# Pair sums of weight tiles made when both raw tiles are rounded, raw tiles rounded seven steps behind their loads, one addition two steps later

## The chip, the cores and the metric

The kernel runs on one core of one Trainium2 chip. A core has five engines that run at once, each with an in-order queue of its own: TensorE (PE, the matmuls), VectorE (DVE), ScalarE (ACT), GpSimd (POOL) and SyncE (SP, which here issues the DMAs). An instruction that waits for another engine or for a DMA holds up all that stands behind it in its queue. The metric is the device time of the program in microseconds.

## The reference

One inference step of one decoder layer: 1024 prompt tokens and 32 sampled tokens, model width 1024, float32. The input projection `p = rmsnorm(x) @ w_in + b_in` feeds two mixers of four heads each (an mLSTM and an HGRN2), an output projection follows, then a gated feed-forward. Cut to what matters here, the HGRN2 half:

```python
fr = f_raw
f = lb + (1.0 - lb) * sigmoid(fr)            # forget gate
kk = (1.0 - lb) * sigmoid(-fr)               # key
q, v = heads(silu(q_raw)), heads(i_raw)
# by chunks of 64 tokens: o = q*exp(b) @ S + (masked, decayed q k^T) @ v;  S carried on
out = headnorm(o) * silu(g_raw)
```

`f_raw`, `q_raw`, `i_raw`, `g_raw` are columns of `p`: for each head h, four weight tiles of 128 columns (f, q, v, g), 1024 rows each.

## The kernel before, in words

**Products.** A float32 product is made of three matmuls of rounded operands: every operand X is kept as `hi` (X rounded to fp32r, which ACT makes) and `lo` (X - hi, the "rest", made by POOL for weight tiles and by DVE for the others), and PE adds hi*hi + hi*lo + lo*hi (lines 179 to 181). A weight tile is 128 x 1024: two halves of 512 columns, each with four k-steps of 128.

**Blocks of tokens.** The tokens lie in three blocks, 0 (288 columns), 1 and 2 (384 each). For heads 0 to 2 of the HGRN2 half, the weights of two tiles (a pair: f and q, or v and g) on blocks 1 and 2 form a 2 x 2 by 2 x 2 block product, which is done with seven products P1 to P7 of four k-steps (twelve matmuls) in place of eight (`strassen_units`). The order on PE is P1, P2, P5, P6, P3, P7, then a plain unit of block 0 with the next pair's first tile (24 matmuls of 288 columns), then P4, then a plain unit with the next pair's second tile. There are six pairs, (h, 0) and (h, 1) for h = 0, 1, 2. P1, P2 and P4 read the rounded raw tiles. P5, P6, P3 and P7 read four sums of raw halves, S1, S2, S4 and S3, each rounded and split like a tile.

**Banks.** The seven products use three PSUM banks: P1 in 0, P2 in 1, P5 in 2, P6 onto bank 0, P3 onto bank 2, P7 and P4 onto bank 0. So P6 must come after the addition that reads P1 (`add`, L1156 from `p2`), P3 after the evacuation of P5 (`p5`, ACT L1152), P7 after that of P6.

**The weights' way.** `load` issues a DMA of a raw tile (512 KB, L105, into one of two buffers "raw"). `split` rounds it on ACT (L96) and has POOL make the rest (L97), half by half. `pairs_split` makes the sums in place in the two raw tiles on DVE (L139, L142, L147, L153), rounds them on ACT (L134), makes their rests on DVE (L137), and loads the next pair's raw tiles into the two buffers as soon as each is free. Rounded tiles and rests have five buffers each (`NW`); a pair takes four, two raw tiles and two tiles of sums.

**The order of the work** is that in which the program is written out. PE's matmuls are emitted unit by unit; after every second k-step and after every unit `hook()` runs one step of each active helper (a Python generator): `split`, `pairs_split`, and `mix_b`, the HGRN2 mixer of a head and a block. A helper's `yield n` puts off its next piece by n steps. So a step is some six matmuls, and a helper's instructions stand in each engine's queue where the step falls. `next_splits(ui)` starts the split of a tile, or `pairs_split`, at the unit that `t_split` gives. In code, `virt` holds the two tiles of sums of a pair with its two raw tiles; `first` and `last_u` are the first and last unit that reads a tile.

`mix_b` builds a chunk's decayed products by doubling levels: DVE multiplies q and k by decays (L865, L867: `qB`, `kB`, `qw`, `ck`) and the decays with each other (L873), DVE puts a level's product into place (L853, L882), PE makes small matmuls (L846, L924, L929), ACT copies (L870, L871, L915). Then PE transposes v and k (L945, L948), ACT and DVE copy them (L954, L955), PE makes the state's update (L964), DVE adds it to the state C (L972, L974), PE makes the output (L984, L986, the latter with C), ACT squares it (L992), and the norm goes on (L551, L556, L997, L1002). A mixer of one block runs while the units of another are multiplied.

Of the kernel before, what the change touches and what calls it, by code (L numbers as in the profile page):

```python
# [13 lines left out]
OP = mybir.AluOpType  # L14
# [26 lines left out]
def hybrid_step(ctx: ExitStack, tc: tile.TileContext, i, o):  # L41
# [18 lines left out]
    def start(gen, key, wait=1):  # L60
        active.append([gen, key, wait])

    def hook():
        for e in list(active):
            e[2] -= 1
            if e[2] > 0:
                continue
            try:
                e[2] = next(e[0]) or 1
            except StopIteration:  # L70
                active.remove(e)
                done.add(e[1])
# [13 lines left out]
    def split(t, pool):  # L86
        while t not in raws or (t and t - 1 not in his):
            yield 1
        hi = his[t] = wp.tile([128, 1024], F32R, tag="whi", name="whi", bufs=NW)
        lo = los[t] = wp.tile([128, 1024], F32R, tag="wlo", name="wlo", bufs=NW)  # L90
        n, raw = tile_n[t], raws[t]
        for c in range(0, n, 512):
            if c:
                yield 2
            s = slice(c, c + 512)
            nc.scalar.activation(hi[:, s], raw[:, s], AF.Copy)  # L96
            (nc.gpsimd if pool else nc.vector).tensor_tensor(lo[:, s], raw[:, s], hi[:, s].bitcast(F32), op=OP.subtract)  # L97
        for x in nexts.get(t, ()):
            load(x)

    tile_n = {}

    def wtile(src, n=1024):
        def f(raw):
# [18 lines left out]
    def pairs_split(tb, ta, raw_a, raw_b):  # L123

        while ("w", raw_b) not in done:
            yield 1
        ra, rb = raws[raw_a], raws[raw_b]
        a11, a12, a21, a22 = ra[:, 0:512], ra[:, 512:1024], rb[:, 0:512], rb[:, 512:1024]

        def rnd(t, s, src):  # L130
            if t not in his:
                his[t] = wp.tile([128, 1024], F32R, tag="whi", name="whi", bufs=NW)
                los[t] = wp.tile([128, 1024], F32R, tag="wlo", name="wlo", bufs=NW)
            nc.scalar.activation(his[t][:, s], src, AF.Copy)  # L134
# [4 lines left out]
        nc.vector.tensor_tensor(a22, a21, a22, op=OP.add)  # L139
# [7 lines left out]
        nc.vector.tensor_tensor(a11, a22, a11, op=OP.subtract)  # L147
# [992 lines left out]
    def swin(h, pair):  # L1140

        n0, n1 = pair
        tags = {"f": ("ngb", 2), "qb": ("cq", 2), "vb": ("v", 2), "g": ("go", 3)}
        bj = {"f": None, "qb": V_BIN + 16 + h, "vb": V_BIN + 24 + h, "g": V_BIN + 28 + h}

        def put(name, b, ps):
            t = S[name, h, b] = tl(tags[name][0], 384, tags[name][1])
            j = bj[name]
            if j is None:
                nc.scalar.activation(t, ps[:, :384], AF.Copy)  # L1150
            else:
                nc.scalar.activation(t, ps[:, :384], AF.Identity, bias=col(j))  # L1152

        def add(name, b, ps):
            t = S[name, h, b]
            nc.vector.tensor_tensor(t, t, ps[:, :384], op=OP.add)  # L1156
# [29 lines left out]
    ts_, virt = {}, {}  # L1186

    def pair_tiles(h, j):
        ta, tb = wtile(wa[17 + 4 * h + 2 * j]), wtile(wa[17 + 4 * h + 2 * j + 1])
        ts_[h, 2 * j], ts_[h, 2 * j + 1] = ta, tb  # L1190
        if h < H - 1:
            for _ in range(2):
                tiles.append(None)
            virt[tb + 1] = (tb + 1, tb + 2, ta, tb)
            virt[tb + 2] = None

    XF = {"P1": (0, 0, "B11"), "P2": (0, 512, "B21"), "P3": (3, 512, "B22"), "P4": (1, 512, "T4"), "P5": (2, 512, "T1"),
          "P6": (3, 0, "T2"), "P7": (2, 0, "T3")}
    for h in range(H):
        for j in range(2):  # L1200
            pair_tiles(h, j)
# [4 lines left out]
    def strassen_units(h, j, posts, mid, end):  # L1206
        evs = swin(h, (("f", "qb"), ("vb", "g"))[j])
        ta = ts_[h, 2 * j]
        for p, bk in (("P1", 0), ("P2", 1), ("P5", 2), ("P6", 0), ("P3", 2), ("P7", 0), ("P4", 0)):
            if p == "P4":  # L1210
                mid()
            d_, coff, b_ = XF[p]
            need = {"P5": "S1", "P6": "S2", "P3": "S4", "P7": "S3"}.get(p)
            unit(ta + d_, (Op(b_, 0), Op(b_, 1)), 4, evs[p], coff=coff, post=posts.get(p), need=need and (need, ta + 2),
                 bank=pmb(bk), acc=p in ("P6", "P3", "P7", "P4"))
        end()

# [702 lines left out]
            nexts[ta] = nexts.pop(ra) + nexts.pop(rb)  # L1920
    t_split, prev = [], 0
    for t in range(n_t1):
        e = max(prev, last_u[t + 1 - NW] + 1 if virt.get(t) else 0, first[t] - 8, last_u[t - NW] + 1 if t >= NW else 0)
        assert e <= first[t], (t, e, first[t])
        t_split.append(e)
        prev = e
# [324 lines left out]
```

## Time and profile before

| what | value |
|---|---|
| median of 3 runs | 1449.21 us (1448.50 to 1449.81) |
| the profiled execution: its time | 1452.79 us |
| the profiled execution: span in the trace | 1451.0 us |
| mean granted PE clock in it | 0.965 |
| PE busy | 1347.2 us, 93% of the span |
| DVE, ACT, POOL busy | 940.0, 584.9, 600.8 us (65%, 40%, 41%) |
| the stage of the six pairs | first sum starts at 294.7 us, last rest of a sum at 517.8 us |
| time on the chain that ended last | PE 69%, DVE 15%, ACT 5%, DMA 5% |

PE is busy nearly all the time over the whole kernel; in the stage of the six pairs it is not, and the shares of the whole span say nothing of that. In the views, a row of waits gives who waited, for whom, us in total, how often and the longest; a row of a timeline gives start, us, engine, line, operation and, in brackets, the idle time before it and what ended it; a row of a tile gives ns at least, in the median and at most.

### The profile page before, as it was taken

The numbers are of one execution on the slowest core, as the hardware profiler recorded it, in microseconds if no ns is written. First come the engines' busy times: TensorE is split into PE (matmuls) and PEld (weight loads), VectorE is DVE, ScalarE is ACT, GpSimd is POOL, SyncE is SP. The second block draws the span as 40 slices with busy tenths as digits, with TensorE's granted clock in tenths as the row PEclk, the third lists the DMA queues.
The fourth block names the chain that finished last, engine by engine and source line by source line (L and its number), as shares of the span: only waits on it lengthen the run. The fifth ranks groups of instructions, "written<-read, shape, count | busy, mean of one in ns | idle before, by whom it ended". The sixth has DMA issues, their size and how long they took to land.

```text
span 1451.0 us, 29523 instructions
## 1 busy us (share of the span) xinstructions
PE 1347.2 (93%) x11528; PEld 1308.4 (90%) x11528; DVE 940.0 (65%) x2158; ACT 584.9 (40%) x1367; POOL 600.8 (41%) x566
## 2 busy tenths in 40 slices
PE   6989999988788879989998999999999999999996
PEld 6878999877788768889998999999999999999995
DVE  6877777665666646664548567756666236777775
ACT  5655444233434334432344444544554341222232
POOL 5323213221211213312345665666566574444434
PEclk9989999999898989999999999999999999999998
DMA  6224323231010133444354666666765258888843
GB/s 217 87 67 152 102 82 93 88 110 39 20 43 20 43 118 139 137 140 147 119 196 125 220 223 236 239 207 218 248 237 191 75 183 330 288 290 282 292 168 120
DMA packets 118724, 229.71 MB, mean 158 GB/s; under 512 B 11680, under 2 KB 72120, under 8 KB 118072
## 3 DMA queue, kind: packets, MB, share of 16 engines
q1 hardware_dynamic: 118152, 227.55, 46.0%
q8 instruction: 91, 1.49, 0.5%
q14 instruction: 49, 0.40, 0.1%
q10 hardware_dynamic: 432, 0.27, 0.1%
HBM read 153.33 MB, written 74.45 MB: 157 GB/s over the span
## 4 chain that ended last, share of the span: by engine, by line
PE 69%; DVE 15%; ACT 5%; DMA 5%; issue 4%; POOL 2%; SPq 0%; POOLq 0%; DVEq 0%; ACTq 0%
PE mx L1524 15%; PE mm L1524 9%; PE mm L179 8%; PE mm L181 8%; PE mm L180 8%; PE mx L1747 7%; PE mm L1747 4%; PE so L1524 3%; DMA raw<-in_wA 2%; DMA rg<-d_ff 2%; PE mx L701 1%; PE mx L846 1%; PE so L1747 1%; ACT whi L96 1%; DVE wlo L137 1%
## 5 line engine op out<-in xcount | busy, mean ns | idle before, releaser
L179 PE MATMUL mm<-HI,whi 128*128 128x384 f32 (+2 forms) x1064 | 348.8, 328 | 17.3 <-ACT go L1152 9.2
L181 PE MATMUL mm<-HI,wlo 128*128 128x384 f32 (+2 forms) x1064 | 334.3, 314 | 1.3 <-POOL wlo L97 1.3
L180 PE MATMUL mm<-LO,whi 128*128 128x384 f32 (+2 forms) x1064 | 334.5, 314 | 0.8 <-DVE LO L1257 0.4
L97 POOL TENSOR_TENSOR wlo<-raw,whi 128x512 fp32r<-128x512 f32 x90 | 120.2, 1344 | 259.7 <-ACT whi L96 215.4
L179 PEld LDWEIGHTS mm<-HI,whi 128*128 128x128 f32 x1064 | 205.7, 193 | 23.9 <-ACT go L1152 10.3
L180 PEld LDWEIGHTS mm<-LO,whi 128*128 128x128 f32 x1064 | 206.1, 194 | 1.9 <-POOL LO L279 0.7
L181 PEld LDWEIGHTS mm<-HI,wlo 128*128 128x128 f32 x1064 | 205.8, 193 | 1.8 <-POOL wlo L97 1.8
L1453 POOL TENSOR_TENSOR wlo<-S,whi 128x512 fp32r<-128x512 f32 x78 | 110.4, 1421 | 89.4 <-ACT whi L1452 84.9
L1524 PE MATMUL mx<-T,whi 128*128 128x264 f32 x640 | 118.2, 284 | 0.0
L1524 PEld LDWEIGHTS mx<-T,whi 128*128 128x128 f32 x640 | 99.0, 188 | 0.0
L1577 POOL TENSOR_TENSOR LO<-rg,HI 128x528 fp32r<-128x528 f32 x52 | 70.6, 1367 | 66.3 <-ACT HI L1576 66.2
L1524 PE MATMUL mx<-HI,whi 128*128 128x264 f32 x320 | 91.1, 285 | 0.2 <-ACT u L1532 0.2
L1524 PE MATMUL mx<-HI,wlo 128*128 128x264 f32 x320 | 90.9, 284 | 0.0
L1524 PE MATMUL mx<-T,wlo 128*128 128x264 f32 x320 | 90.9, 284 | 0.0
L1524 PE MATMUL mx<-LO,whi 128*128 128x264 f32 x320 | 90.7, 283 | 0.0
L1665 DVE TENSOR_TENSOR fh<-fr,fh 128x512 fp32r<-128x512 f32 x80 | 68.0, 850 | 34.0 <-ACT fh L1660 33.7
L1751 DVE TENSOR_TENSOR X<-X,mx 128x264 f32<-128x264 f32 x160 | 65.5, 425 | 26.9 <-PE mx L1747 26.3
L1452 ACT ACTIVATE whi<-S 128x512 fp32r<-128x512 f32 x80 | 50.3, 630 | 71.0 <-DVE S L1441 67.2
L1576 ACT ACTIVATE HI<-rg 128x528 fp32r<-128x528 f32 x52 | 32.3, 641 | 105.1 <-PE mx L1747 31.7
L96 ACT ACTIVATE whi<-raw 128x512 fp32r<-128x512 f32 x90 | 54.2, 622 | 50.1 <-DMA raw<-in_wA 50.1
L1524 PE MATMUL mm<-HI,wlo 128*128 128x264 f32 x240 | 68.2, 284 | 0.0
L1524 PE MATMUL mm<-HI,whi 128*128 128x264 f32 x240 | 68.2, 284 | 0.0
(584 smaller groups left out, 3684.7 us busy)
## 6 DMA issues: line engine op xcount, KB each, us to landing
d_wf<-fh SPq DMA_DIRECT2D x60, 512.0 KB
rg<-d_ff SPq DMA_DIRECT2D x42, 528.0 KB
raw<-in_wA SPq DMA_DIRECT2D x31, 512.0 KB
whi<-d_wf SPq DMA_DIRECT2D x29, 512.0 KB
wlo<-d_wf SPq DMA_DIRECT2D x28, 512.0 KB
raw<-in_wgu SPq DMA_DIRECT2D x24, 512.0 KB
d_ff<-sg SPq DMA_DIRECT2D x40, 264.0 KB
rg<-in_wgu SPq DMA_DIRECT2D x20, 512.0 KB
```

What stands on the lines that cost most here:

```text
L96: nc.scalar.activation(hi[:, s], raw[:, s], AF.Copy)
L97: (nc.gpsimd if pool else nc.vector).tensor_tensor(lo[:, s], raw[:, s], hi[:, s].bitcast(F32), op=OP.subtract)
L179: nc.tensor.matmul(ps[:, :n], wh, rh[:, k, :], start=(k == 0 and not u["acc"]), stop=False, skip_group_check=sk)
L180: nc.tensor.matmul(ps[:, :n], wh, rl[:, k, :], start=False, stop=False, skip_group_check=sk)
L181: nc.tensor.matmul(ps[:, :n], wl, rh[:, k, :], start=False, stop=(k == nk - 1), skip_group_check=sk)
L1452: nc.scalar.activation(hi[:, s], t, AF.Copy)
L1453: (nc.vector if dve else nc.gpsimd).tensor_tensor(lo[:, s], t, hi[:, s].bitcast(F32), op=OP.subtract)
L1524: nc.tensor.matmul(ps[:, :QN], a[:, w], b_[:, kk, c], start=new and kk == 0 and x == 0, stop=kk == 3 and x == 2, skip_group_check=True)
L1577: (nc.vector if dve else nc.gpsimd).tensor_tensor(lw, src, h.bitcast(F32), op=OP.subtract)
L1665: nc.vector.tensor_tensor(lw, src, h.bitcast(F32), op=OP.subtract)
L1747: nc.tensor.matmul(ps[:, :QN], a[:, w], b_[k][:, cs], start=new and k == 0 and x == 0, stop=k == 1 and x == 2, skip_group_check=True)
L1751: nc.vector.tensor_tensor(y, y, ps[:, :QN], op=OP.add)
```

## The change

It moves instructions; none is added or taken away, and the same values are computed.

- `pairs_split` is started by `split` of the pair's second raw tile, as soon as that is rounded, and makes all four sums then. It waits for a mark ("free", tile), which `next_splits` sets where it started `pairs_split` before, and only then rounds the sums, in the order S2, S4, S1, S3 (S1, S2, S4, S3 before). S2 and S4 lie in the first of the two tiles of sums now, S1 and S3 in the second.
- `hook` counts its calls. The two loads that `pairs_split` issues note the count plus 7 in `landed`, and `split` rounds such a tile no earlier than at that count.
- the addition that reads P1 is started two steps after P2's evacuation instead of with it.

```diff
     def hook():
+        hooks[0] += 1
...
     def split(t, pool):
         while t not in raws or (t and t - 1 not in his):
             yield 1
+        while hooks[0] < landed.get(t, 0):
+            yield 1
...
         for x in nexts.get(t, ()):
             load(x)
+        if virt.get(t + 2):
+            start(pairs_split(*virt[t + 2]), ("w", t + 2))
...
         nc.vector.tensor_tensor(a22, a21, a22, op=OP.add)
         yield 1
-        rnd(tb, right, a22)
         nc.vector.tensor_tensor(a21, a11, a21, op=OP.subtract)
         yield 1
-        rest(tb, right, a22)
-        done.add(("S1", tb))
-        yield 1
         nc.vector.tensor_tensor(a11, a22, a11, op=OP.subtract)
+        yield 1
+        nc.vector.tensor_tensor(a12, a12, a11, op=OP.subtract)
+        yield 1
+        while ("free", tb) not in done:
+            yield 1
         rnd(ta, left, a11)
         yield 1
         rest(ta, left, a11)
         done.add(("S2", tb))
-        yield 1
-        nc.vector.tensor_tensor(a12, a12, a11, op=OP.subtract)
         rnd(ta, right, a12)
         yield 1
         rest(ta, right, a12)
         done.add(("S4", tb))
         x0, x1 = nexts[ta]
         load(x0)
-        yield 1
+        landed[x0] = hooks[0] + 7
+        rnd(tb, right, a22)
+        yield 1
+        rest(tb, right, a22)
+        done.add(("S1", tb))
         rnd(tb, left, a21)
...
         load(x1)
+        landed[x1] = hooks[0] + 7
...
         def p2(ps):
             put(n0, 1, ps)
-            add(n0, 1, pm[0])
+            start(later(n0, pm[0]), ("later", n0, h), 2)
...
             if nxt in virt:
-                if virt[nxt]:
-                    start(pairs_split(*virt[nxt]), ("w", nxt))
+                done.add(("free", nxt))
```

The order on PE is the same, instruction by instruction. Three places in the other queues, first ACT in pair (0,1), from P2's evacuation on. `whi<-raw` of L134 rounds a sum, of L96 a raw tile; `v<-mm` and `go<-mm` evacuate P2, P5 and P6. Before:

```order
L96 ACTIVATE whi<-raw 128x512
L1152 ACTIVATE v<-mm,vec 128x384
L134 ACTIVATE whi<-raw 128x512
L870 ACTIVATE qw<-qB 128x24x8
L871 ACTIVATE ck<-kB 128x24x8
L96 ACTIVATE whi<-raw 128x512 x2
L1152 ACTIVATE go<-mm,vec 128x384
L992 ACTIVATE kt,sm<-mx 128x128 x2
L96 ACTIVATE whi<-raw 128x512
L1152 ACTIVATE v<-mm,vec 128x384
```

After the change, where L101 rounds a raw tile, L1163 evacuates, L881, L882 and L1003 are L870, L871 and L992 of before, L926 is L915, and L814 and L815 make the next block's key `ck` and gate `ngb`:

```order
L1163 ACTIVATE v<-mm,vec 128x384
L881 ACTIVATE qw<-qB 128x24x8
L882 ACTIVATE ck<-kB 128x24x8
L1163 ACTIVATE go<-mm,vec 128x384
L101 ACTIVATE whi<-raw 128x512
L1003 ACTIVATE kt,sm<-mx 128x128 x2
L1163 ACTIVATE v<-mm,vec 128x384
L926 ACTIVATE AT_124<-AD_126 32x3x32 x4
L101 ACTIVATE whi<-raw 128x512 x2
...
L815 ACTIVATE ngb<-ngb,vec 128x384
L101 ACTIVATE whi<-raw 128x512
```

The evacuations of P2 and P5 now stand ahead of the first rounding of a raw tile, and the last of the four roundings stands behind `ngb`.

The DVE near the end of the same pair, from the addition of P3 on (`v<-v,mm`); `go<-go,mm` adds P7, and `qB`, `kB` are the mixer's last level, which PE's L948 transposes. Before:

```order
L1156 TENSOR_TENSOR v<-v,mm 128x384
L807 TENSOR_SCALAR ngb<-ngb,omlb,lb 128x384
L808 TENSOR_SCALAR ck<-ck,omlb 128x384
L1156 TENSOR_TENSOR go<-go,mm 128x384
L865 TENSOR_TENSOR qB<-qB,wib 128x3x64
L867 TENSOR_TENSOR kB<-kB,wib 128x3x64
```

After, with L146, L148 and L150 three of the four sums of the next pair:

```order
L1167 TENSOR_TENSOR v<-v,mm 128x384
L818 TENSOR_SCALAR ngb<-ngb,omlb,lb 128x384
L819 TENSOR_SCALAR ck<-ck,omlb 128x384
L146 TENSOR_TENSOR raw<-raw 128x512
L1167 TENSOR_TENSOR go<-go,mm 128x384
L876 TENSOR_TENSOR qB<-qB,wib 128x3x64
L878 TENSOR_TENSOR kB<-kB,wib 128x3x64
L884 TENSOR_TENSOR wib<-wib 128x3
L148 TENSOR_TENSOR raw<-raw 128x512
L150 TENSOR_TENSOR raw<-raw 128x512
```

The sums have come in between the mixer's instructions of the pair before, the first of them ahead of `go`, `qB` and `kB`.

The DVE in pair (1,0), around the addition that reads P1 (`ngb<-ngb,mm`); L137 and L144 make the rest of a sum. Before, as the piece between the mixer's level ahead and the copy of `kt`:

```order
L137 TENSOR_TENSOR wlo<-raw,whi 128x512
L153 TENSOR_TENSOR raw<-raw 128x512
L137 TENSOR_TENSOR wlo<-raw,whi 128x512
L1156 TENSOR_TENSOR ngb<-ngb,mm 128x384
L865 TENSOR_TENSOR qB<-qB,wib 128x3x64
L867 TENSOR_TENSOR kB<-kB,wib 128x3x64
L873 TENSOR_TENSOR wib<-wib 128x3
L137 TENSOR_TENSOR wlo<-raw,whi 128x512
```

After:

```order
L144 TENSOR_TENSOR wlo<-raw,whi 128x512
L876 TENSOR_TENSOR qB<-qB,wib 128x3x64
L878 TENSOR_TENSOR kB<-kB,wib 128x3x64
L884 TENSOR_TENSOR wib<-wib 128x3
L1167 TENSOR_TENSOR ngb<-ngb,mm 128x384
L966 COPY kt<-mx 128x384
```

The products `qB` and `kB` no longer stand behind the addition.

More of the change, by code (lines that the diff above doesn't have):

```diff
@@ L61, in start @@
         active.append([gen, key, wait])
+    hooks, landed = [0], {}
     def hook():
+        hooks[0] += 1
         for e in list(active):
@@ L99, in split @@
             load(x)
-    tile_n = {}
+        if virt.get(t + 2):
+            start(pairs_split(*virt[t + 2]), ("w", t + 2))
+    tile_n, virt = {}, {}
     def wtile(src, n=1024):
@@ L140, in pairs_split @@
         yield 1
-        rnd(tb, right, a22)
         nc.vector.tensor_tensor(a21, a11, a21, op=OP.subtract)
         yield 1
-        rest(tb, right, a22)
-        done.add(("S1", tb))
+        nc.vector.tensor_tensor(a11, a22, a11, op=OP.subtract)
         yield 1
-        nc.vector.tensor_tensor(a11, a22, a11, op=OP.subtract)
+        nc.vector.tensor_tensor(a12, a12, a11, op=OP.subtract)
+        yield 1
+        while ("free", tb) not in done:
+            yield 1
         rnd(ta, left, a11)
@@ L1166, in p2, with later @@
             put(n0, 1, ps)
-            add(n0, 1, pm[0])
+            start(later(n0, pm[0]), ("later", n0, h), 2)
+        def later(name, ps):
+            add(name, 1, ps)
+            return
+            yield
         def p5(ps):
@@ L1184, in swin @@
         return {"P1": lambda ps: None, "P2": p2, "P5": p5, "P6": p6, "P3": p3, "P7": p7, "P4": p4}
-    ts_, virt = {}, {}
+    ts_ = {}
     def pair_tiles(h, j):
@@ L1193, in pair_tiles @@
                 tiles.append(None)
[L1194 to L1198, printed above, removed]
+            virt[tb + 1] = None
+            virt[tb + 2] = (tb + 2, tb + 1, ta, tb)
+    XF = {"P1": (0, 0, "B11"), "P2": (0, 512, "B21"), "P3": (2, 512, "B22"), "P4": (1, 512, "T4"), "P5": (3, 512, "T1"),
+          "P6": (2, 0, "T2"), "P7": (3, 0, "T3")}
     for h in range(H):
@@ L1213, in strassen_units @@
             need = {"P5": "S1", "P6": "S2", "P3": "S4", "P7": "S3"}.get(p)
-            unit(ta + d_, (Op(b_, 0), Op(b_, 1)), 4, evs[p], coff=coff, post=posts.get(p), need=need and (need, ta + 2),
+            unit(ta + d_, (Op(b_, 0), Op(b_, 1)), 4, evs[p], coff=coff, post=posts.get(p), need=need and (need, ta + 3),
                  bank=pmb(bk), acc=p in ("P6", "P3", "P7", "P4"))
@@ L1922, in hybrid_step @@
     for t in range(n_t1):
-        e = max(prev, last_u[t + 1 - NW] + 1 if virt.get(t) else 0, first[t] - 8, last_u[t - NW] + 1 if t >= NW else 0)
+        e = max(prev, last_u[t + 1 - NW] + 1 if t in virt and not virt[t] else 0, first[t] - 8, last_u[t - NW] + 1 if t >= NW else 0)
         assert e <= first[t], (t, e, first[t])
```

## The prediction

> **What bounds the kernel now.** Two views come first: how often the tensor engine (PE) is busy, and whom it waits for. The change touches only the stage in which six pairs of weight tiles are multiplied by seven products, between 295 and 531 us. The waits of PE from 309 to 531 us (waiter, releaser, us in total, times, longest):
>
> ```profile
> PE mx L948 <- DVE kB L867: 11.9, 2, 6.0
> PE mm L179 <- ACT go L1152: 9.2, 3, 4.0
> PE mx L986 <- DVE C L972: 8.6, 3, 2.9
> PE mm L179 <- DVE cq L532: 4.7, 1, 4.7
> ...
> PE mm L179 <- ACT ngb L804: 1.1, 1, 1.1
> ```
>
> The first four groups make 34.4 us, and the releasers named are evacuations and products of the mixer, not the weights. So the next question is what held ScalarE (ACT) and VectorE (DVE) up. ACT's first wait from 286 to 560 us, by length:
>
> ```profile
> ACT whi L96 <- DMA raw<-in_wA: 49.2, 11, 5.6
> ```
>
> ACT waits 11 times, 4.5 us each, for a weight tile that is still on its way (L96 rounds a raw tile). The chain of waits shows one such place, in the pair that ends at 448 us (start, us, what):
>
> ```profile
> 429.83 3.25 DMA raw<-in_wA
> ...
> 433.11 0.63 ACT whi L96
> 433.74 0.48 ACT v L1152
> 434.21 0.02 issue
> 434.24 0.55 DVE v L1156
> 434.79 0.21 DVE C L972
> ...
> 437.83 3.45 DMA raw<-in_wA
> ...
> 441.84 0.57 ACT go L1152
> 442.42 0.04 issue
> 442.46 0.69 PE mm L179
> ```
>
> The last rest (L137) of a raw tile frees its buffer, the load of the next tile goes out and takes 3.3 us (3.5 the second time), and ACT's queue already has that tile's rounding at its head. Everything behind it (v, go, then on the DVE v and C) waits with it. **The bound of this stage is a load in the middle of two in-order queues**, twice in each pair. In six windows around these places (start:end, us; busy us and instructions of PE, weight loads, DVE, ACT, POOL; granted PE clock):
>
> ```profile
> 309.70:327.00 17.30, 11.44 (x84) 10.20 (x83) 11.24 (x32) 9.50 (x25) 6.86 (x7) 0.80 0.24 79
> 352.10:368.00 15.90, 10.45 (x99) 9.21 (x99) 7.70 (x26) 8.10 (x22) 6.17 (x6) 0.79 0.17 54
> 391.50:404.30 12.80, 6.53 (x65) 5.50 (x63) 5.11 (x10) 3.96 (x10) 3.93 (x4) 0.73 0.25 82
> 431.80:448.60 16.80, 11.26 (x87) 9.84 (x87) 8.30 (x26) 8.09 (x22) 6.83 (x6) 0.70 0.14 46
> 472.30:486.10 13.80, 7.87 (x71) 7.16 (x70) 5.64 (x12) 4.74 (x11) 5.13 (x5) 0.75 0.23 76
> 511.00:530.00 19.00, 12.08 (x91) 10.95 (x91) 8.17 (x26) 8.09 (x22) 6.17 (x6) 0.75 0.33 107
> ```
>
> The windows last 95.6 us together and PE is busy in 59.6 of them: **36.0 us idle**. The clock is low too. Busy time times (1 - clock), window by window, is 2.3 + 2.2 + 1.8 + 3.4 + 2.0 + 3.0 = **14.6 us**. What the twelve loads cost is thus up to 50.6 us.
>
> **The change part by part.**
>
> *Later rounding of raw tiles.* A raw tile is now rounded at least seven steps behind its load. A step is six matmuls of a product, and six of 384 columns take 1.17 us at full clock (368.43 to 369.60):
>
> ```profile
> 368.43 0.45 PE L179 MATMUL mm<-HI,whi 128*128 128x384 f32 x1
> ...
> 369.60 0.29 PE L179 MATMUL mm<-HI,whi 128*128 128x288 f32 x1
> ```
>
> Seven steps are about 8 us against the 3.3 us of a load, so I let all eleven waits of L96 go. The order of ACT after the change bears it out: v and go, which stood behind the rounding, stand ahead of it. Gain: the 50.6 us, less what takes its place.
>
> *Pair sums early.* The same four sums, 24 roundings and 24 rests are done, with the same tiles loaded, so busy time does not change. The sums move to before the pair and overwrite the raw tile, so the first of them (L146 in the change) must wait for POOL's last rest of that tile. That is a **new wait in the middle of the DVE's queue**. Its rows:
>
> ```profile
> L97 POOL TENSOR_TENSOR wlo<-raw,whi x25: 1262/1281/1565, 287.0 to 526.2; 128x512 fp32r<-128x512 f32 x25
> ...
> L139 DVE TENSOR_TENSOR raw<-raw x6: 683/1092/1494, 294.7 to 501.0; 128x512 f32<-128x512 f32 x6
> ```
>
> In pairs (0,1) and (1,1) the sum of the next pair stands ahead of the go addition and the products qB, kB for which PE's L948 waits. I follow ACT and PE from the end of product P6 (call it 0). The rows of before for (0,1):
>
> ```profile
> 363.75 0.59 ACT L1152 ACTIVATE v<-mm,vec 128x384 f32<-128x384 f32 x1
> 364.21 1.14 ACT L915 ACTIVATE AT<-AD 32x96 f32<-32x96 f32 x4
> ...
> 366.53 0.62 ACT L804 ACTIVATE ngb<-ngb,vec 128x384 f32<-128x384 f32 x1
> ...
> 369.80 0.56 DVE L1156 TENSOR_TENSOR go<-go,mm 128x384 f32<-128x384 f32 x1 [1.70 <-PE mm L181]
> ...
> 370.54 0.35 DVE L867 TENSOR_TENSOR kB<-kB,wib 128x192 f32<-128x192 f32 x1
> ...
> 367.78 0.34 PE L924 MATMUL mx<-qw,ck 128*32 128x32 f32 x9
> ...
> 371.04 0.52 PE L948 MATMUL mx<-ident,kB 128*128 128x128 f32 x3 [0.16 <-DVE wib L873]
> ```
>
> ACT: v 0.59, AT 1.14, two roundings 1.26 (0.63 each, by L96 in the chain), two copies about 0.7, ck and ngb 1.24 (0.62 each), the last rounding 0.63: 5.6. POOL's rest 1.28: 6.9. DVE: sum 0.68, go 0.56, qB and kB 0.7 (0.35 each): 8.8. PE: 18 matmuls 3.5, then from L924 to L948 as before, 371.04 - 367.78 = 3.26 less its wait of 0.16, 3.1: 6.6, at which it wants L948. **The new wait is about 2.2 us**, and 0.4 us of it would be there without the sum (ACT's ngb is done at 4.9; its scaling on the DVE, about 0.9 as two such instructions, and go and the products follow: 7.0). Bounds: 0, if POOL is done when ACT is, and 6.1 if three queued rests of 1.28 follow each other first. What does such a wait cost in clock? The 2.85 us waits at L986 (the third row above) were followed, the first time, by these two windows:
>
> ```profile
> 355.50:358.00 2.50, 2.49 (x53) 2.06 (x56) 2.43 (x10) 1.15 (x3) 0.20 (x2) 0.71 0.03 7
> 358.00:362.50 4.50, 2.28 (x25) 1.92 (x17) 0.27 (x1) 0.77 (x2) 1.41 (x2) 0.78 0.39 117
> ```
>
> 2.49 x 0.29 + 2.28 x 0.22 = 1.2 us were lost behind 2.85 us of wait. I take 1.2 (and 0 as the other end), so 3.4 us at each of two places: **6.8 back**, between 0 and 14.6. Pair (2,1) has no sums ahead: **0.4 back**.
>
> The Trainium skill, "TensorE: Matmul & The Clock Gate", section "Why this matters for your kernels", says that only gaps of more than about 3 us bring the clock down. The row of 355.5 us speaks against it, with 0.71 granted after 2.85 us. By the rule the two places would give back 4.4 instead of 6.8 us, and the time would be 2.4 us lower than mine.
>
> In pairs (0,0), (1,0), (2,0) the sums stand between the mixer's level products, POOL's four rests run beside them, and a sum next to POOL took 1.49 us instead of 0.68 (row L139). No row shows how much of this reaches PE. I take one sum ahead of the products and one such stretch, 0.68 + 0.81 = 1.5 us per place, **4.5 back**, between 0 (PE's slack covers it) and 9 (twice that).
>
> *Rounding of sums in the order S2, S4, S1, S3.* P5 needs S1, now third. The three roundings stand back to back with inputs long ready, where before ACT and DVE passed each sum to and fro. Three roundings and three rests need some 3.9 us (0.63 and, like a sum, 0.68 each) and P5 is two products (24 matmuls, 4.7 us) away: nothing. If that cover were gone it would be one rounding and one rest, 1.3 us a pair.
>
> *One addition two steps later.* P6 accumulates onto the bank that it reads, so it must be done before P6. It has 1.17 us of P5's second half and the mixer's matmuls for its 0.55 us: nothing; uncovered, 0.55 us a pair, 3.3 in all.
>
> *Loads.* Both loads of a pair go out earlier, with the same bytes. On SP they pass one store of states in (0,0); nobody waits for it there.
>
> *What stays in pair (0,0).* P5 waited 4.7 us for cq (fourth wait above), the end of a DVE chain that starts with ACT's ngb. ACT before:
>
> ```profile
> 310.12 0.63 ACT L96 ACTIVATE whi<-raw 128x512 fp32r<-128x512 f32 x1 [4.52 <-DMA raw<-in_wA]
> ...
> 312.46 0.49 ACT L804 ACTIVATE ngb<-mm,vec 128x288 f32<-128x288 f32 x1
> ```
>
> ck and ngb read a product that lies on PE just ahead of P1. PE's wait for ngb (1.1 us, fifth row above) came after P1, whose twelve matmuls take 2.3 us, and ended with ngb at 312.95; so the product was there by 312.95 - 1.1 - 2.3 = 309.6, before the load was. Without the rounding ahead of them, ck and ngb (0.49 and as much) are done at 310.6, some 2.3 us sooner, and with a rounding of sums (0.63, behind ngb in ACT's queue) moved forward too the chain is some 2.7 sooner. PE arrives 1.1 us sooner as well, so 4.7 - 2.7 + 1.1 = 3.1 us of wait stay, and with them I leave 1.5 of that window's 2.3 us of clock: **4.6 back**, between 3 and 7.
>
> **Sum.** 50.6 - 6.8 - 0.4 - 4.5 - 4.6 = 34.3 us. The profiled execution took 1452.8 us (span 1451.0), which gives 1418.5 for one like it; it stands 3.6 us above the median of the runs, 1449.2, so the forecast is **1415 us**. With all that comes back at its least (3) the gain is 47.6, 1401.6; at its most (14.6 + 1 + 9 + 7 = 31.6) it is 19, 1430.
>
> **The rivals.**
>
> *The waits just vanish:* POOL is done in time and PE meets nothing new, 1402 us or a little less. For it: none of PE's long waits names a weight tile. Against it: ACT's queue is full from P6 to the last rounding. 0.14.
>
> *DVE behind POOL becomes the next bound:* the sum's wait is twice mine, the level products slip at every pair, and PE pays clock again. The gain falls to 10 to 25 us, 1424 to 1439. For it: the DVE is the busiest of the helpers in the six windows, 46 us against ACT's 42. 0.16.
>
> *The change doesn't do what it says:* steps are counted, not time, and a step can pass without a matmul when a wait is being filled; then the rounding still meets its load, and the time stays at 1449. Against it: PE's order is the same instruction by instruction. 0.04.
>
> *Slower:* the same wait of the DVE's sum for POOL, at the five places where sums stand, (0,0) to (2,0), costs more than it frees. It decides from 50.6 / 5 = 10.1 us a place; at 12 us (POOL held by PE's old tiles, PE by the DVE behind it) the time is 1449.2 + 9.4 = 1459. Against it: the upper bound above is 6.1. 0.04.
>
> **How the numbers follow.** My forecast (gain 25 to 44) has 0.58, the rivals 0.14, 0.16, 0.04 and 0.04, and 0.04 is left for a gain beyond 50. About 0.2% is what a measurement can tell from no change. Faster by more than that: 0.58 + 0.14 + 0.16 + 0.04 = 0.92; within 0.04; slower 0.04. The range takes the bounds of the unknown costs and reaches a little into the second rival: 1401 to 1434.
>
> **What the profile after would show.** ACT's waits for raw tiles from in_wA between 286 and 530 us: near 0 instead of 49 us. L986 waiting for C and the main matmuls for go: gone. L948 waiting for kB: about 2 us in (0,1) and (1,1), none of 6 us in (1,0) and (2,0), with the sum waiting for POOL just ahead. P5 of (0,0) still waiting some 3 us for cq. The clock in the stretches of the six windows near 0.9 or above. If ACT still waits for loads, the first step is wrong; if a wait for POOL of over 5 us stands on the DVE at each sum, the second.

## The result and the profile after

| what | before | changed |
|---|---|---|
| median (runs of one comparison) | 1448.86 us (1447.89 to 1449.81) | 1411.99 us (1411.00 to 1413.13) |
| ratio to before | | 0.9746, interval 0.9729 to 0.9763 |
| the profiled execution: its time | 1452.79 us | 1411.00 us |
| mean granted PE clock | 0.965 | 0.98 |
| PE busy | 1347.2 us (93%) | 1331.9 us (95%) |

The forecast was 1415 us, 1401 to 1434. By medians the change saves 36.9 us; the two profiled executions differ by 41.8, because that of before lies 3.9 us above its median and that of the change 1.0 below.

The first step was that no rounding of a raw tile waits for its load. The view of line L101 (L96 before) in the changed kernel, from 286 to 530 us, gives the roundings and then, under "until", what its engine sat idle for; before, it was the DMA for 49.2 us:

```profile
L101 ACT ACTIVATE whi<-raw x30: 613/622/669, 308.0 to 522.6; 128x512 fp32r<-128x512 f32 x30
its engine sat idle before it (us, times) until:
who waited for it (us, times):
```

The list under "until" is empty. PE's waits after the change, 286 to 540 us (waiter, releaser, us, times, longest; L959 is L948 of before, L940 L929, L857 L846):

```profile
PE mx L959 <- DVE wib L884: 7.5, 3, 2.9
PE mx L940 <- DVE wib L884: 3.1, 2, 1.6
PE mx L857 <- DVE wib L884: 2.9, 4, 1.0
PE mx L940 <- ACT qB L881: 2.0, 2, 1.0
PE mx L857 <- ACT sg L1172: 1.6, 3, 0.7
```

PE's waits for go and cq are gone, and C is down from 8.6 to 0.9 us. L959 still waits for kB (`wib` L884 is the small product behind it): 2.86 us in (0,1), 2.87 in (1,1), 1.80 in (2,1).

PE's order is the same in both kernels, so the start of one and the same matmul can be compared. How far the change is ahead, worked out from the two timelines of PE (starts before and after, us):

| up to | before | after | ahead by | gained or given back |
|---|---|---|---|---|
| first pair's sums | 296.86 | 295.18 | 1.7 | |
| end of window 1, (0,0) | 325.69 | 315.27 | 10.4 | +8.7 |
| start of (0,1) | 334.63 | 325.92 | 8.7 | -1.7 |
| end of window 2 | 366.81 | 348.91 | 17.9 | +9.2 |
| behind L959's wait | 374.47 | 362.01 | 12.5 | -5.4 |
| end of window 3, (1,0) | 408.05 | 387.07 | 21.0 | +8.5 |
| start of (1,1) | 417.90 | 398.73 | 19.2 | -1.8 |
| end of window 4 | 448.07 | 418.87 | 29.2 | +10.0 |
| behind L959's wait and the next pair's start | 469.61 | 444.78 | 24.8 | -4.4 |
| end of window 5, (2,0) | 482.66 | 450.01 | 32.7 | +7.8 |
| start of (2,1) | 498.53 | 466.95 | 31.6 | -1.1 |
| end of window 6 | 530.15 | 487.10 | 43.1 | +11.5 |
| behind L959's wait | 533.85 | 492.44 | 41.4 | -1.6 |

The six places of the loads give 55.7 us, and 16.0 come back between them: 39.7 in this stage. Predicted were 50.6 and 16.3. Neither sum holds what lies ahead of the first row. Up to 290 us, where nothing differs, the two executions are already 2.8 us apart; 1.1 of that are lost at 295 us, where PE's L602 waits 1.0 us for the DVE, a wait that is found neither in the kernel before nor in the one with the delay alone.

Where the most comes back, in (0,1), the timeline of the changed kernel (start, us, engine, line, operation, and in brackets the idle time before it and what ended it):

```profile
346.91 0.58 ACT L1163 ACTIVATE v<-mm,vec 128x384 f32<-128x384 f32 x1 [1.98 <-PE mm L192]
...
351.39 0.61 DVE L818 TENSOR_SCALAR ngb<-ngb,omlb,lb 128x384 f32<-128x384 f32 x1 [1.84 <-ACT ngb L815]
...
351.93 1.53 DVE L819 TENSOR_SCALAR ck<-ck,omlb 128x384 f32<-128x384 f32 x1
351.96 1.28 POOL L102 TENSOR_TENSOR wlo<-raw,whi 128x512 fp32r<-128x512 f32 x1 [0.17 <-ACT whi L101]
...
353.20 1.11 POOL L886 TENSOR_TENSOR qw<-cq,ngb 128x384 f32<-128x384 f32 x1
353.38 1.48 DVE L146 TENSOR_TENSOR raw<-raw 128x512 f32<-128x512 f32 x1
...
355.51 0.35 DVE L878 TENSOR_TENSOR kB<-kB,wib 128x192 f32<-128x192 f32 x1
...
356.00 0.87 PE L959 MATMUL mx<-ident,kB 128*128 128x128 f32 x3 [2.86 <-DVE wib L884]
```

From the end of P6 (346.9) the last rest of POOL ends at 6.3 (6.9 predicted), kB at 8.95 (8.8), and L959 wanted it at 6.2 (6.6). The time that the DVE lost is not written as a wait for POOL, though: ck's scaling takes 1.53 us where its median is 0.42, and ends 0.2 us behind POOL's rest; the sum takes 1.48 where its median is 0.69, and ends 0.55 us behind POOL's L886, as if it had begun only then. What the wait costs behind it, by the granted clock of the same kernel (start:end, us; busy of PE, weight loads, DVE, ACT, POOL; clock):

```profile
356.00:358.00 2.00, 2.00 (x53) 1.63 (x54) 1.49 (x3) 0.25 (x1) 0.00 (x0) 0.50 0.04 8
358.00:360.00 2.00, 2.00 (x10) 2.00 (x10) 1.99 (x6) 0.67 (x2) 0.00 (x0) 0.50 0.00 0
360.00:362.00 2.00, 2.00 (x10) 1.99 (x9) 0.81 (x3) 0.00 (x0) 0.00 (x0) 0.50 0.00 0
```

Six busy microseconds at a granted clock of 0.50 lose 3 us, by the same estimate that had given me 1.2.

### The profile page after: what moved, and what is told of

Same layout as the page of the kernel before. It is cut to its first block, busy times and chain, and to the rows that moved or that the text cites. A ratio compares the mean times of both kernels' runs of the same rounds, so it can differ in the third digit from the quotient of the medians.

```text
span 1409.2 us, 29523 instructions
## 1 busy us (share of the span) xinstructions
PE 1331.9 (95%) x11528; PEld 1297.2 (92%) x11528; DVE 935.5 (66%) x2158; ACT 582.7 (41%) x1367; POOL 601.6 (43%) x566
## 4 chain that ended last, share of the span: by engine, by line
PE 69%; DVE 16%; ACT 7%; issue 4%; POOL 2%; DMA 2%; POOLq 0%; ACTq 0%; DVEq 0%; SPq 0%
PE mx L1540 16%; PE mm L1540 9%; PE mx L1763 8%; PE mm L190 7%; PE mm L192 7%; PE mm L191 7%; PE mm L1763 5%; PE so L1540 3%; ACT whi L101 1%; PE so L1763 1%; PE mx L712 1%; DMA rg<-d_ff 1%; PE mx L857 1%; POOL LO L1593 1%; ACT HI L294 1%
## 5 line engine op out<-in xcount | busy, mean ns | idle before, releaser
L1469 POOL TENSOR_TENSOR wlo<-S,whi 128x512 fp32r<-128x512 f32 x78 | 109.7, 1411 | 92.3 <-ACT whi L1468 89.2
L1681 DVE TENSOR_TENSOR fh<-fr,fh 128x512 fp32r<-128x512 f32 x80 | 66.5, 832 | 34.3 <-ACT fh L1676 34.1
L567 POOL TENSOR_TENSOR sm<-sm,mhalf 128x3 f32<-128x3 f32 (+2 forms) x26 | 23.0, 883 | 106.6 <-DVE sm L562 73.6
```

Source lines behind the costliest of these rows:

```text
L1469: (nc.vector if dve else nc.gpsimd).tensor_tensor(lo[:, s], t, hi[:, s].bitcast(F32), op=OP.subtract)
L1681: nc.vector.tensor_tensor(lw, src, h.bitcast(F32), op=OP.subtract)
```

## The experiments

Medians and ratios are to the kernel before, measured on the same chip in the same comparison. The changed kernel's interval is 0.9729 to 0.9763.

**The parts alone.** First the delay without the early sums: `landed` and the wait in `split` are put into the kernel before, and nothing else.

```diff
     def hook():
+        hooks[0] += 1
...
         while t not in raws or (t and t - 1 not in his):
             yield 1
+        while hooks[0] < landed.get(t, 0):
+            yield 1
...
         load(x0)
+        landed[x0] = hooks[0] + 7
...
         load(x1)
+        landed[x1] = hooks[0] + 7
```

> The kernel before, with only the raw tiles rounded seven steps behind their loads; the sums are still made inside the pair, in the old order. Theory A (the load at the head of ACT's queue was the cost): ACT's 49 us of waits for in_wA go to near 0, the waits of PE for go (L179, 9.2 us) and C (L986, 8.6) go, and the time is 1411 to 1420. Theory B (the delay needs the early sums as well: without them the roundings of the sums, each waiting for the DVE, 25 us in all, still stand between the evacuations, and the next pair's sums now start later): the waits for in_wA go, but PE waits for rounded sums or raw tiles instead, and the time is 1425 to 1445.

Measured: 1407.26 us, ratio 0.9713 (0.9699 to 0.9728). No wait for in_wA is left, nor one for go, and C is down to 0.9 us. Theory A holds in its waits, and B falls; the time is below the range that A gave (1411 to 1420). The delay alone is worth 41.5 us, more than the whole change. Together, the other edits cost some 5 us: the two intervals only just do not touch, but the matched matmuls of the two traces give 4.9 us from 270 to 540 us as well. One wait of the change is there without any early sum (L955 is L948 of before, L874 makes kB), 1.5 us in each of (0,1), (1,1) and (2,1):

```profile
PE mx L955 <- DVE kB L874: 4.5, 3, 1.5
```

Next the other edits without the delay (`+ 7` becomes `+ 0`, at both loads):

> The changed kernel with the 7 set to 0: sums early, in the new order, and no delay. Theory A: raw tiles are again rounded while their load of 3.3 us is on its way, ACT waits for in_wA by 30 to 50 us in some 11 waits, and the time is 1432 to 1450. Theory C (the early sums and the earlier loads carry the gain, since the loads go out sooner anyway): ACT waits for in_wA by under 15 us, 1410 to 1420.

Measured: 1430.96 us, ratio 0.9879 (0.9859 to 0.9898), a little below A's range and far from C's. ACT's row, which is below A's 30 to 50 us in 11 waits and above C's 15:

```profile
ACT whi L101 <- DMA raw<-in_wA: 23.0, 6, 4.4
```

Half of the waits are back (23.0 us in 6 of 49.2 in 11). The early sums and loads remove the other half alone, so they and the delay do in part the same thing: 17.8 and 41.5 us one by one, 36.9 together.

The addition back in its old place, with P2's evacuation:

```diff
-            start(later(n0, pm[0]), ("later", n0, h), 2)
+            add(n0, 1, pm[0])
```

> The changed kernel with the addition that reads P1 started with P2's evacuation, as before. My prediction costed this edit at nothing: within 1.5 us of the changed kernel (ratio to before within 0.001 of 0.9746). Rival: the products qB and kB behind the addition in pairs (h,0) make PE wait about 0.55 us each, 1.7 us in all, up to 3.3 us slower with clock.

Measured: 1415.47 us (1411.43 to 1415.86), ratio 0.9762 (0.9745 to 0.9779). The median is 3.5 us above that of the change, outside the 1.5 that I had allowed and nearer to the rival's 1.7 to 3.3, but the intervals overlap, and the trace does not bear the rival out. L959 waits for kB five times instead of three (8.5 us instead of 7.5); even so, this kernel is 3.0 us late against the changed one ahead of the stage, where nothing differs, and 2.6 at 493 us. It loses 1.5 us at one place behind that. In (2,1) L959 waits 1.80 us in the changed kernel and 1.79 in this one, and only in this one does the clock fall behind that wait. First the changed kernel, then this one:

```profile
494.00:496.00 2.00, 2.00 (x17) 2.00 (x16) 1.80 (x6) 0.65 (x2) 0.00 (x0) 1.00 1.02 406
```

```profile
497.00:499.00 2.00, 2.00 (x10) 1.99 (x9) 0.93 (x3) 0.63 (x2) 0.00 (x0) 0.50 1.02 427
```

So neither the times nor the traces tell what this edit brings here from nothing.

The same edit added to the kernel with the delay alone:

> The kernel before with the delay of seven steps and the addition that reads P1 two steps later, without the early sums. If that edit is worth about 1 us in the traces (0.3 us for each of L936 and L955 in three pairs), the time is 1405 to 1407; if nothing, 1407.3 as with the delay alone, within 1.5 us; if P6 now waits for the addition, 1409 or more.

Measured: 1413.08 us, ratio 0.9742 (0.9721 to 0.9763), above the 1407.3 without it, though the intervals touch (that one ends at 0.9728). The trace names a cost, though the matched matmuls show only 1.7 us of it by 540 us:

```profile
PE mm L186 <- DVE v L1163: 2.8, 3, 0.9
```

In (h,1) P6 now waits 0.9 us for the addition. Where sums are still rounded inside the pair, the DVE has a rest of 0.68 us ahead of it, and the cover that I had counted on is not there. Whether the edit costs nothing depends on the others.

**The sum ahead of kB.** In the changed kernel the sums start one step later:

```diff
-            start(pairs_split(*virt[t + 2]), ("w", t + 2))
+            start(pairs_split(*virt[t + 2]), ("w", t + 2), 2)
```

> The changed kernel with the sums started one step later; in pairs (0,1) and (1,1) the first sum then stands behind kB on the DVE, with nothing else in that stretch moved. Theory A (the sum itself, 1.48 us beside POOL, is half of L959's wait): L959's waits at the two places fall from 2.86 us to about 1.8, as in pair (2,1), where there is no sum; 2 x 1.06 us and some 1 us of clock each, so 2 to 5 us faster than the changed kernel. Rival (the wait is set by ACT's ngb and the DVE's scaling, the sum only fills time in which POOL blocks the DVE anyway): the waits stay above 2.5 us and the time within 1.5 us.

Measured: 1404.93 us, ratio 0.9693 (0.9679 to 0.9706): 7 us faster than the change, more than expected. L959's waits, and the clock behind those of (0,1) and (1,1):

```profile
PE mx L959 <- DVE wib L884: 5.3, 3, 1.8
```

```profile
358.70:360.70 2.00, 2.00 (x11) 1.98 (x10) 1.58 (x4) 0.67 (x2) 0.00 (x0) 0.50 0.00 0
...
425.30:427.30 2.00, 2.00 (x17) 2.00 (x16) 2.00 (x6) 0.72 (x3) 0.00 (x0) 1.00 0.00 0
```

The waits fall to 1.73 and 1.80 as expected. Beyond that, L857's waits for sg (1.6 us) are gone, and behind (1,1) the clock stays at 1.00. The edit starts all four sums of every pair a step later, so more than one instruction has moved: in the matched matmuls it gains 4.8 us at L959's waits in (0,1) and (1,1) and 2.0 at the starts of (0,1), (1,1) and (2,1). The place of the sums thus accounts for what the early sums had cost. It does not account for the whole of L959's wait: with no sum ahead, qB and kB took 0.96 and 1.14 us in (0,1) and ck's scaling 1.52 in (1,1), all beside POOL.

**The size of the delay.** Nine steps in place of seven, at both loads; in the runs after it 12, 4 and 5 stand there:

```diff
-        landed[x0] = hooks[0] + 7
+        landed[x0] = hooks[0] + 9
...
-        landed[x1] = hooks[0] + 7
+        landed[x1] = hooks[0] + 9
```

> The changed kernel with 9 in place of 7. Two of the three roundings ahead of ngb in ACT's queue then stand behind it, the first sum stands behind kB, and POOL's rests fall behind ngb's and ck's scaling on the DVE. Theory A (L959's waits of 2.86, 2.87 and 1.80 us come from ACT's roundings ahead of ngb, 0.6 us each, from ck's scaling that took 1.53 us beside POOL's rest instead of some 0.5, and from the sum): the three waits fall below 1 us each, 6 us less in all with 2 to 4 us of clock, 1400 to 1405. Rival (POOL's rests only move: they slow the DVE elsewhere, and the sums that come later hold the next pair): L959's waits fall, others of the same size come up at L857, L940 or for rounded weights, and the time stays within 2 us of the kernel with the sums one step later (1405) or goes above it.

Measured: 1411.72 us (1407.33 to 1414.92), ratio 0.9737 (0.9713 to 0.9761), not told apart from seven; its runs lie 7.6 us apart. Theory A falls, and the time is the rival's. The rival's reason is seen in part: POOL's rests do slow the DVE elsewhere, but no waits of the size of L959's come up at L857 and L940 (10.1 us in all instead of 11.4). In the matched matmuls the stage is even 2.5 us shorter than with seven; that the medians do not show it stays open. In (1,1) the first sum is out of the way, and this stands in its place:

```profile
418.99 2.74 POOL L102 TENSOR_TENSOR wlo<-raw,whi 128x512 fp32r<-128x512 f32 x2 [0.90 <-ACT whi L101]
...
420.52 1.42 DVE L878 TENSOR_TENSOR kB<-kB,wib 128x192 f32<-128x192 f32 x1
```

qB and kB, 0.35 us each without POOL, take 0.70 and 1.42; kB ends 0.2 us behind the second of POOL's two rests, and L959 waits 1.58 us where I had expected less than 1.

Twelve steps:

> The changed kernel with 12 in place of 7: all roundings of raw tiles but one stand behind ngb. Theory A: L959's waits below 0.5 us, as with 9, but raw tiles and sums now come late for the next pair, where POOL's four rests of 1.28 us stand among the level products; 1400 to 1410. Rival (later is always better up to the point where a tile is missing): below the run with 9 by 2 us or more.

Measured: 1410.15 us, ratio 0.9726 (0.9711 to 0.974). The time is at the upper end of what A gave, but the reason is not A's: L959 waits 8.4 us in 3 and 1.9 once, not under 0.5. Later is not always better, so the rival falls too.

Four steps:

> The changed kernel with 4 in place of 7. Four steps are 4.7 us against a load of 3.3 us. Theory A (the delay works by time, so that the load has landed): ACT waits for in_wA under 6 us in all, PE's waits for go and C do not come back, and the time is 1400 to 1415. Rival (the delay works by place: what matters is that the roundings stand behind the evacuations v and go): the roundings stand ahead of them again, and the time is 1418 to 1430 though no load is waited for.

Measured: 1402.4 us, ratio 0.9678 (0.9662 to 0.9695), 9.6 us faster than the change. ACT waits 5.0 us for in_wA, 4 times. PE does not wait for go, and 0.9 us in all for C. In (0,1) two roundings stand ahead of the evacuation of P5 in ACT's queue again, and now cost no wait:

```profile
343.88 1.14 ACT L101 ACTIVATE whi<-raw 128x512 fp32r<-128x512 f32 x2
344.98 0.58 ACT L1163 ACTIVATE go<-mm,vec 128x384 f32<-128x384 f32 x1
```

Theory A holds: the delay works by time, not by the place ahead of or behind the evacuations, and seven steps are more than it needs.

Four steps in the kernel before, with the late sums:

> The kernel before with a delay of four steps, without the early sums and the other two edits. It stands against the delay of seven alone (1407) and the changed kernel with four (1402). If the early sums bring nothing of themselves, it is within 2 us of 1402. If the gain of four over seven in the changed kernel came from the sums' place (the first two of them ahead of the scaling of ngb, in time in which the DVE waited for ACT), four is no better than seven here: 1405 to 1410. If the load is not landed after four steps without the early loads, ACT waits for in_wA by over 10 us and the time is over 1412.

Measured: 1408.41 us (1403.12 to 1410.9), ratio 0.9712 (0.9694 to 0.973): no better than seven there. So what four steps gain over seven comes with the early sums. In the timeline with four steps three of them stand on the DVE ahead of ngb's scaling, where it had waited 1.84 us for ACT, and no rest of POOL runs beside ck's scaling; that this is the whole of the gain is argued from those places and was not tried apart.

Five steps in the changed kernel:

> The changed kernel with 5 in place of 7, between the best run so far (4: 1402.4) and the change (7: 1412.0). Two sums stand ahead of the scaling of ngb and ck and a third one behind it, ahead of go and kB; all roundings stand ahead of ngb. By theory D, no rest of POOL runs beside ck's scaling, qB or kB, but the third sum (0.68 us) stands ahead of kB: L959's waits about 1.5 us in (0,1) and (1,1), under 0.5 in (2,1), 1401 to 1406. Rival (time grows evenly with the delay, about 3 us a step): 1405 to 1407.

Measured: 1407.73 us, ratio 0.9716 (0.9702 to 0.9729), above my range and just above the rival's. In (1,1) a wait appears that I had predicted for the change:

```profile
417.17 0.62 ACT L815 ACTIVATE ngb<-ngb,vec 128x384 f32<-128x384 f32 x1
417.52 0.69 DVE L146 TENSOR_TENSOR raw<-raw 128x512 f32<-128x512 f32 x1 [1.52 <-POOL wlo L102]
...
419.19 0.48 DVE L818 TENSOR_SCALAR ngb<-ngb,omlb,lb 128x384 f32<-128x384 f32 x1
```

The first sum waits 1.52 us for POOL's last rest at the head of the DVE's queue, and the scaling behind it starts 1.4 us after ngb was ready (417.79). L959 waits 2.17 us.

**POOL beside the DVE.** In the changed kernel the rests of the pairs' raw tiles go to the DVE:

```diff
-                start(split(nxt, True), ("w", nxt), {3: 3, 4: 10}.get(nxt, 1))
+                start(split(nxt, nxt + 2 not in virt and nxt + 1 not in virt), ("w", nxt), {3: 3, 4: 10}.get(nxt, 1))
```

> The changed kernel with the rests of the pairs' raw tiles made by the DVE instead of POOL (20 of them, 0.7 us each instead of 1.28). ACT's and PE's order is the same, on the DVE each rest stands where its rounding is written. Theory D (a DVE instruction that meets a rest on POOL stands still until that ends: ck's scaling 1.53 us and the sum 1.48 us, instead of 0.4 and 0.68): both are back at 0.4 and 0.7 us, a rest of 0.7 is added ahead of the sum, so L959's waits fall from 2.86 and 2.87 to about 1.8 and from 1.80 to 1.2; without the half clock behind the first two the time is 1404 to 1410. Rival (the long durations are the DVE's own, or the DVE has no room for 14 us more): the durations stay above 1.2 us, or L959's and L940's waits grow, and the time is 1413 to 1422.

Measured: 1406.02 us, ratio 0.9698 (0.9685 to 0.9712), 6 us faster although the DVE has more to do. The timeline of (0,1):

```profile
353.34 0.41 DVE L819 TENSOR_SCALAR ck<-ck,omlb 128x384 f32<-128x384 f32 x1
353.59 1.63 POOL L886 TENSOR_TENSOR qw<-cq,ngb 128x384 f32<-128x384 f32 x1 [7.18 <-ACT AT L946]
353.67 0.68 DVE L146 TENSOR_TENSOR raw<-raw 128x512 f32<-128x512 f32 x1
```

ck's scaling and the sum are back at 0.41 and 0.68 us, as theory D has it, and L959 waits 0.93 us, in (1,1) 0.90. The edit does not reach (2,1), where POOL still makes the rests of the tiles that come after the pairs: there ck's scaling takes 1.52 us beside one of them, as in the changed kernel, and L959 waits 1.77, not the 1.2 that I had expected. So the place that was left alone stays as it was, and the two that were changed are free of it. Two waits of 1.45 us at L940 are new, behind two rests on the DVE. This time POOL's L886 is the long one, 1.63 us instead of 1.11. The Trainium skill, "SBUF — State Buffer", section "SBUF: two separate sides", says that GpSimd shares a pair of ports with the DVE as an exclusive lock, against DVE instructions in a two-port mode or with two inputs in SBUF: whichever starts first holds it for its whole instruction and the other is blocked. The rows agree with both sides of that (the DVE at 1.53, 1.48 and 1.42 us, POOL at 1.63); they show the long instructions, not the ports.

Four steps and the rests on the DVE together:

> The changed kernel with 4 in place of 7 and the rests of the pairs' raw tiles on the DVE. With 4 alone (1402.4) PE's L857 still waits 1.2 us each at two places for kB, behind a qB that took 1.42 us beside POOL's rest instead of 0.35. Theory D: qB is back at 0.35 us and these two waits fall to about 0.8 (a rest of 0.7 us may stand ahead), L959's stay about 1 us; 1399 to 1403. Rival (the DVE's 14 us more now lie on the path elsewhere, as at L940 with rests on the DVE and a delay of 7, where two waits of 1.45 us were new): 1404 to 1409.

Measured: 1400.88 us (1400.17 to 1404.72), ratio 0.9673 (0.9656 to 0.9691): the fastest median of all, but not told apart from four steps alone (in the matched matmuls its stage is 2.8 us longer). L959's waits fall from 2.3 to 1.7 us in all. Of the two waits of L857 for kB one is gone. In (1,1) the DVE makes the rest, qB is back at 0.35 us, and PE does not wait. In (2,1) the rest belongs to a tile after the pairs, which the edit leaves on POOL; there qB stays long, and L857 waits 1.21 us as before:

```profile
403.54 0.35 DVE L876 TENSOR_TENSOR qB<-qw,wib 128x192 f32<-128x192 f32 x1
...
467.42 1.32 POOL L102 TENSOR_TENSOR wlo<-raw,whi 128x512 fp32r<-128x512 f32 x1 [2.82 <-ACT whi L101]
467.53 1.43 DVE L876 TENSOR_TENSOR qB<-qw,wib 128x192 f32<-128x192 f32 x1
```

Theory D holds where the edit reaches. Other waits of L857 take the gain back (one of 1.1 us in (0,0), and 1.9 instead of 0.7 for sg): 6.7 us in all instead of 5.8. Both medians lie 10 to 11 us under that of the change, with intervals wholly below its own.

## Why the prediction was right, step by step

**The bound, right.** A load at the head of an in-order queue held ACT, and with it the DVE and PE. The delay alone shows it: 41.5 us for a counter and a wait that only move roundings, and no wait for in_wA left. Without the delay 23.0 us of these waits are back, and 19 us of time with them. With a delay of four steps roundings stand ahead of an evacuation again and cost no wait there, so it was the load, not the rounding itself.

**The gain of the six places, 50.6, a little low.** The matched matmuls gave 55.7. With the delay alone the same six stretches give 49.9, close to what I had counted for it, and 5.1 come back. The other 5.8 thus came with the rest of the change, 5.5 of them in (0,0), (1,0) and (2,0); the prediction had no term for that, and which edit brought them was not tried apart.

**The new wait of L959, right in place and about right in size, wrong in what it is made of, its price too small.** Predicted 2.2 us, measured 2.86 and 2.87; with the clock 3.4 a place predicted, 5.4 and 4.4 measured (the second with the start of the next pair), 9.8 instead of 6.8 in all. The clock behind it was taken from a stretch at 0.71 to 0.78, and it was 0.50.

Of the 2.2 us I gave 1.8 to the sum and 0.4 to what would be there without it. With no sum ahead 1.73 and 1.80 us were left, and with the delay alone 1.50 and 1.50. With the rests off POOL and the sum in its place 0.93 and 0.90 were left. So the sum made about 1.1 us, and POOL's rests beside the DVE the larger part, by long instructions that my sum of terms did not have: ck's scaling at 1.53 us, where I had 0.9 for both scalings. That the total came near is luck. I also had the sum standing idle until POOL's rest ended; that wait showed only with five steps.

In (2,1) I had 0.4 us, and 1.80 was measured (1.6 by the table): there is no sum there, but ck's scaling took 1.52 us beside POOL's rest. The run with the rests on the DVE left POOL's in (2,1) as they were, and kept both.

**The sums among the mixer's levels, 4.5 predicted, 4.6 measured** at the starts of (0,1), (1,1) and (2,1). With the delay alone nothing is lost there (0.0, 0.0 and a gain of 0.7 us), so the loss does come with the early sums. A part is seen. In (1,0), three sums stand close together on the DVE from 393.15 us on (L148, L150 and L152; the last is shown):

```profile
394.60 0.69 DVE L152 TENSOR_TENSOR raw<-raw 128x512 f32<-128x512 f32 x1
...
396.90 1.05 ACT L926 ACTIVATE AT<-AD 32x64 f32<-32x64 f32 x4 [3.60 <-DVE AD L864]
...
398.73 0.61 PE L940 MATMUL mx<-qB,kB 128*32 128x64 f32 x8 [0.98 <-ACT qB L881]
```

AD comes 2 us late, ACT waits for it with qB behind it, and PE waits 0.98 us for qB. Such waits (2.0 in 2 for qB, 1.6 in 3 for sg) make 3.6 us. For the last microsecond I have no row, and POOL had no part in these rows, so the 0.81 us of contention in my term was not what cost the time here: that the total agrees is in part luck.

**Pair (0,0), wrong: 4.6 us were to stay, none did.** The step that failed is the place of the product that ck and ngb read. I had "the product was there by 309.6", worked back from P1, and used that bound as the time. After the change ck starts as soon as its product ends, and cq follows long before P5:

```profile
299.31 1.28 ACT L814 ACT_TABLE_LOAD   x1
303.47 0.50 ACT L814 ACTIVATE ck<-mm,nbf 128x288 f32<-128x288 f32 x1 [2.88 <-PE mm L192]
...
310.73 0.51 DVE L543 SCALAR_TENSOR_TENSOR cq<-mm,vec,cq 128x288 f32<-128x288 f32 x1
```

The last matmul of that product is the same one in both kernels, and in the kernel before it ended at 305.04: the product lies a whole plain unit ahead of P1, not just ahead of it. So ck, which ran at 312.06, had been held back by 7.0 us, not by 2.3. The last 1.28 us of them are a row of the kernel before that my view left out, between the rounding and ck:

```profile
310.77 1.28 ACT L803 ACT_TABLE_LOAD   x1
```

This load too had stood behind the rounding; with the change it runs while ACT waits for the product. cq came 8.8 us sooner, and the wait went.

**The edits at nothing.** The later addition brought nothing that the times or traces can tell, and costs 0.9 us at three places in a kernel without the early sums. The order S2, S4, S1, S3 was not tried alone; PE waits for no rounded sum after the change, so it cost nothing that shows, and what it gained is not shown either.

**The sum.** 50.6 less 16.3 was 34.3 us; the stage gave 55.7 less 16.0, 39.7, in the traces, and the medians 36.9. What was gained came out 5.1 us higher than predicted. What comes back agrees by luck, for two errors went against each other: 4.6 that did not stay, and 4.2 more at the three waits of L959 (9.8 and 1.6 instead of 6.8 and 0.4).

**The rule on the clock.** By the Trainium skill, "TensorE: Matmul & The Clock Gate", section "Why this matters for your kernels", these gaps of under 3 us would have kept the clock, and the forecast would have been 2.4 us lower, 1412.6. The median is close to that, but not for this reason: the clock did fall, to 0.50 for 6 us.

## What to carry to other kernels

Where an in-order queue reads a tile that is still being loaded, put the reader behind the load by the load's time and little more: in the changed kernel four steps, 4.7 us against a load of 3.3, were better than five, seven, nine or twelve, though with the late sums four were no better than seven. Each step of delay also moves what follows from the reader (here POOL's rests) onto other work. A part of a change that looks harmless because it adds no work should be run alone: here one edit gave all of the gain and the rest gave some back, until the sums were started one step later. And an instruction on the critical queue that takes several times its usual duration can be a wait in disguise; look at what the neighbouring engine was doing until it ended.

## What the runs showed of the hardware that I had not expected

PE's clock after a short gap is not settled by the gap's length alone. It was 0.50 for about 6 us after a wait of 2.86 us in the changed kernel. It was 0.50 after one of 1.79 us with the addition back in its place, and 1.00 after one of 1.80 us in the changed kernel, at the same matmul. With the delay alone it was 1.00 after two waits of 1.50 us and fell below 0.6 after one of 1.48 us. What decides between them stays open.

The DVE and POOL hold each other up: a product of 0.35 us took 1.42 beside a rest on POOL and was back at 0.35 when that rest left POOL, and POOL's product of 1.11 us took 1.63 beside the DVE. Not every DVE instruction is held: with the delay alone, the addition of P7 (go<-go,mm), which has one input in PSUM, took its usual 0.55 us beside a rest of POOL.
